# Squared-ReLU MLP's second half: quarter sums issued further ahead, left operands made in three steps, later weights' loads moved ahead and onto two queues

## The chip, the cores and the metric

The kernel runs on one core of one Trainium2 chip. A time is the device time of one execution in microseconds (us); the kernel before took 2211.32 us (median of 3 runs, 2208.41 to 2215.10). The core's engines are named as the profile names them: PE multiplies matrices (PEld loads its weights), DVE adds and subtracts, ACT copies, casts and applies functions, POOL here does little but issue DMAs, SP issues DMAs. Every engine has a queue of its own and works through it in order.

## The reference

One decoder layer on x of 512 rows by 2048 columns, all in float32:

```python
u = x * (1.0 + sc1) + sh1
y = _mixer(u, ...)                       # gated linear attention and mLSTM heads
x = _layer_norm(ALPHA * x + g1 * y, ln1_g, ln1_b)
u = x * (1.0 + sc2) + sh2
y = jnp.square(jax.nn.relu(u @ w_ff1)) @ w_ff2      # 2048 -> 8192 -> 2048
x = _layer_norm(ALPHA * x + g2 * y, ln2_g, ln2_b)
```

sh, sc and g come from the conditioning vector. The change is in the second product of the MLP, h² @ w_ff2, where h² is 512 by 8192 and w_ff2 is 8192 by 2048, and in the last steps of the first product, beside which the second one is begun.

## The kernel before

The layer is computed stage by stage: modulation, mixer, output projection and first norm; the MLP's first product, whose squared results go to DRAM (`hd`); the MLP's second product; the last norm. Float32 operands are split into two reduced-precision parts, hi and lo (lo is the operand less hi), and a product is three matmuls: hi by hi, hi by lo, lo by hi.

**The sevens.** The first twelve blocks of 512 hidden rows ("fours") are multiplied by a Strassen-Winograd scheme: a block of four quarter products is replaced by seven products of sums of quarters. The twelve fours are worked off in nine *runs* (runs 0 to 8), of 2, 3, 3, 3, 3, 3, 3, 3 and 1 fours and with the two halves of the output columns in turn. A run goes through seven *passes*, in the order of products 1, 2, 5, 7, 3, 6, 4 (`PASS`), and a pass takes each four of its run in turn. One four in one pass is a *unit*: 12 matmuls of 128x512 (`seven`, L1531 to L1538). There are NU = 168 units. A pass collects in two PSUM banks; after it ACT copies both to SBUF (`evac`, L1560, two copies) and a DMA adds them to `sums` in DRAM: the first time written by SP, then added by POOL (L1564).

**What a unit needs.** From the weights: the four quarters of a four come by SP (`quarter_load`, 512 KB each, L1315, into two rings of six). `right_operand` is called two units ahead of the matmuls (LOOK = 2). For products 5, 7, 6 and 4 it first has DVE make a sum of quarters in place (L1327), then ACT casts it to hi (L1330), then the pending subtractions are issued (`low_parts`), and the subtraction for this unit's lo (DVE, L1332) is put on the list `lows`, to be issued by the next call. hi and lo stand in rings of three. From the activations: `left_operand` makes two DVE sums for products 5 (L1292, L1293) and 3 (L1295, L1296), at once the ACT cast to hi (L1299), and puts the DVE subtraction for lo (L1300) on the same list. `WHEN` says in which pass each left operand is made, one step per unit.

**Order.** DVE and ACT run in the order in which the program calls them; PE, SP and POOL are ordered by a scheduler. At unit n the loop therefore puts on DVE, in this order: the sum of quarters for unit n + 2, if it wants one, the lo of unit n + 1, and what left operands are due; ACT gets the cast of unit n + 2, the left casts, and after a pass the two copies.

**The end of the first product.** After the last block of the first product, DVE and ACT combine seven PSUM banks (L1472 to L1488, seven DVE operations of 128x512), then apply relu and square (`waiting`, L1492) and store to `hd`. The quarters of run 0 are loaded there, and the first two fours' left operands are made beside it (`beside_last`).

**The plain part.** The other hidden rows: 24 *plain units* of 24 matmuls, in four column blocks C0 to C3 of six units (L1546 to L1548; weights loaded by `c_load`, L130, into a ring `raw` of three buffers that the activations `hr` also pass through, split by `split`, L125 on ACT and L126 on DVE). In C0 the sums of the sevens are read back from DRAM (`sums_load`, L1574, called q) and combined (`z_sums`). Then 192 matmuls of `last_sum`, the last norm, and the output.

Of the kernel before, what the change touches and what calls it, by code (L numbers as in the profile page):

```python
# [58 lines left out]
def trunk_layer_kernel(  # L59
# [1227 lines left out]

    def left_operand(f, k):
# [8 lines left out]
        src = q[{1: (1, 1), 2: (1, 2), 5: (2, 1), 7: (1, 1), 3: (1, 2), 6: (1, 1), 4: (2, 2)}[m]]
        h, l = (slot(HOME[kind_of(f)][1], f"a{f}_{m}{e}") for e in "hl")
        A.copy(halves(h), src)  # L1299
        lows.append(lambda: V.tensor_tensor(halves(l), src, halves(h), ALU.subtract))  # L1300
        left[f, m] = h, l
# [79 lines left out]
    WHEN = {"a": (1, 1, 4, 4, 7, 8, 8), "b": (4, 4, 7, 7, 8, 8, 8), "c": (4, 4, 4, 7, 7, 8, 8)}  # L1381

    def spread(r, k, fns):
        fs = len(runs[r])
        for i, fn in enumerate(fns):
            at(at_pass(r, k) + i * fs // len(fns), fn)
# [62 lines left out]
    for nb in range(2, DFF // CB):  # L1449
# [120 lines left out]
    def sums_load(h, j, q, k):  # L1570
# [185 lines left out]
```

## Time and profile before

| | us |
| --- | --- |
| median of 3 runs | 2211.32 (2208.41 to 2215.10) |
| the profiled execution, its own time | 2206.32 |
| its span in the trace | 2204.6 |
| PE busy in the span | 2111.1 (96%) |
| DVE busy in the span | 1718.5 (78%) |
| ACT busy in the span | 961.9 (44%) |
| sevens, runs 0 to 8 (1487.75 to 2006.88) | 519.13 |
| plain blocks C0 to C3 (2006.88 to 2147.86) | 140.98 |
| last sums and norm (from 2147.86) | 56.7 |

The span is what the trace covers; the execution's own time is 1.7 us longer, and the median of the three runs is 5.0 us above that execution. A row of a wait says which instruction stood idle, which instruction released it, the sum of these waits, their number and the longest. A row of a timeline says when an instruction began, how long it took from start to end (the next one can begin a little before that end, so the distance of two starts is what a queue pays), and in brackets how long its engine had been idle and what ended it.

### The profile page before, as it was taken

The page shows a single profiled execution, that of the slowest core. Times are in us where ns is not written, and L with a number is a line of the kernel's source. Part 1 is how long each engine was busy: PE and PEld are TensorE (multiplying, and loading weights), DVE is VectorE, ACT ScalarE, POOL GpSimd, SP SyncE. Part 2 cuts the span into 40 slices and gives each one's busy share as a digit, 9 for nine tenths or more (in the row PEclk, how much of TensorE's full clock was granted, in tenths as well). Part 3 has the DMA queues.
Part 4 walks back from the last instruction along what each step waited for, and adds up shares of the span by engine and source line. Part 5 has one row for each costly group of instructions (what it writes and reads, how often), then busy time and mean ns, then how long its engine had stood idle before and what let it go on. Part 6 is the DMA issues. An engine that isn't in the chain of part 4 may idle for free.

```text
span 2204.6 us, 30720 instructions
## 1 busy us (share of the span) xinstructions
PE 2111.1 (96%) x11857; PEld 1826.7 (83%) x11857; DVE 1718.5 (78%) x2550; ACT 961.9 (44%) x1328; POOL 166.1 (8%) x156
## 2 busy tenths in 40 slices
PE   6999999999999999999999999997999899998997
PEld 4777788888888879999999999995777687777786
DVE  7985777577777788987888878877777877775888
ACT  4223643343331145544544545445555555553233
POOL 3334101000000000000000000000001010001002
PEclk9999999999999999999999999999999999999999
DMA  8875444766678866444443444447467677769652
GB/s 312 285 266 172 137 144 147 245 201 228 223 256 290 287 204 201 131 139 123 143 128 113 154 125 129 140 155 273 171 175 185 175 196 176 192 169 262 220 179 79
DMA packets 187120, 415.04 MB, mean 188 GB/s; under 512 B 17105, under 2 KB 19373, under 8 KB 186973
## 3 DMA queue, kind: packets, MB, share of 16 engines
q1 hardware_dynamic: 179916, 387.38, 53.2%
q0 software_dynamic: 7056, 25.69, 7.0%
q8 instruction: 93, 1.52, 0.3%
q14 instruction: 55, 0.44, 0.1%
HBM read 354.74 MB, written 58.21 MB: 187 GB/s over the span
## 4 chain that ended last, share of the span: by engine, by line
PE 69%; DVE 14%; DMA 8%; ACT 5%; issue 3%; POOL 0%; SPq 0%; ACTq 0%; DVEq 0%; POOLq 0%
PE fp L1461 8%; PE fp L1460 8%; PE fp L1462 8%; PE gp L1537 4%; PE gp L1538 4%; PE gp L1536 4%; DMA wr<-in_w_ada_dram 3%; DVE wr L162 3%; DVE w L1327 2%; PE gp L1547 1%; PE gp L1548 1%; PE gp L1546 1%; PE wo_0b L228 1%; PE wo_0b L230 1%; PE wo_0b L229 1%
## 5 line engine op out<-in xcount | busy, mean ns | idle before, releaser
L162 DVE SCALAR_TENSOR_TENSOR wr<-wr,csb 128x1024 f32<-128x1024 f32 x192 | 257.7, 1362 | 24.2 <-DMA wr<-in_w_ada_dram 24.0
L1564 POOL DMA_DIRECT2D sums<-z x49 | 42.2, 861 | 1132.6 <-ACT z L1560 1120.1
L1327 DVE TENSOR_TENSOR w<-w,w 128x1024 f32<-128x1024 f32 x96 | 116.9, 1217 | 0.0
L1560 ACT COPY z<-gp 128x512 f32<-128x512 f32 x126 | 70.5, 587 | 26.5 <-PE gp L1538 14.5
L1169 DVE TENSOR_TENSOR z<-f 128x512 f32<-128x512 f32 x112 | 76.7, 685 | 3.1 <-DMA f<-in_w_ff_dram 3.1
L1332 DVE TENSOR_TENSOR w_3lo<-w,w_3hi 128x1024 fp32r<-128x1024 f32 x24 | 29.4, 1225 | 36.7 <-ACT w_3hi L1330 36.7
L1332 DVE TENSOR_TENSOR w_1lo<-w,w_1hi 128x1024 fp32r<-128x1024 f32 x24 | 29.4, 1225 | 29.4 <-ACT w_1hi L1330 27.9
L1492 ACT ACTIVATE z<-z 128x1024 f32<-128x1024 f32 x28 | 28.1, 1053 | 54.6 <-DVE z L1487 54.6
L1171 DVE TENSOR_TENSOR z<-f,z 128x256 f32<-128x256 f32 x112 | 47.6, 425 | 3.9
L1172 DVE TENSOR_TENSOR z<-f,z 128x256 f32<-128x256 f32 x112 | 47.6, 425 | 3.8
L1536 PE MATMUL gp<-w_5hi,a_5h 128*128 128x512 f32 x96 | 38.2, 424 | 8.7 <-ACT w_5hi L1330 8.7
L1537 PE MATMUL gp<-w_5lo,a_5h 128*128 128x512 f32 x96 | 39.8, 415 | 6.6 <-DVE w_5lo L1332 6.6
L1537 PE MATMUL gp<-w_6lo,a_6h 128*128 128x512 f32 x96 | 38.4, 400 | 5.3 <-DVE w_6lo L1332 5.3
L1536 PE MATMUL gp<-w_3hi,a_3h 128*128 128x512 f32 x96 | 37.8, 398 | 5.4 <-ACT w_3hi L1330 5.4
L1536 PE MATMUL gp<-w_4hi,a_4h 128*128 128x512 f32 x96 | 37.8, 397 | 5.1 <-ACT w_4hi L1330 5.1
L1330 ACT CAST w_5hi<-w 128x1024 fp32r<-128x1024 f32 x24 | 25.2, 1051 | 37.2 <-DVE w L1327 37.2
L1537 PE MATMUL gp<-w_2lo,a_2h 128*128 128x512 f32 x96 | 38.5, 402 | 2.8 <-DVE w_2lo L1332 2.8
L1330 ACT CAST w_6hi<-w 128x1024 fp32r<-128x1024 f32 x24 | 25.3, 1052 | 34.7 <-DVE w L1327 34.7
L1536 PE MATMUL gp<-w_7hi,a_7h 128*128 128x512 f32 x96 | 37.7, 394 | 2.5 <-ACT w_7hi L1330 2.5
L1538 PE MATMUL gp<-w_5hi,a_5l 128*128 128x512 f32 x96 | 39.2, 409 | 0.0
L1537 PE MATMUL gp<-w_4lo,a_4h 128*128 128x512 f32 x96 | 37.6, 391 | 1.1 <-DVE w_4lo L1332 1.1
L1537 PE MATMUL gp<-w_7lo,a_7h 128*128 128x512 f32 x96 | 37.6, 391 | 1.1 <-DVE w_7lo L1332 1.0
(1849 smaller groups left out, 8024.2 us busy)
## 6 DMA issues: line engine op xcount, KB each, us to landing
wr<-in_w_ada_dram SPq DMA_DIRECT2D x192, 512.0 KB, 4.7
f<-in_w_ff_dram SPq DMA_DIRECT2D x136, 512.0 KB, 3.7
w<-in_w_ff_dram SPq DMA_DIRECT2D x96, 512.0 KB, 6.5
sums<-z POOLq DMA_DIRECT2D x49, 512.0 KB, 6.5
hd<-z SPq DMA_DIRECT2D x32, 512.0 KB, 4.1
z<-hd SPq DMA_DIRECT2D x12, 1024.0 KB, 7.4
sums<-z SPq DMA_DIRECT2D x14, 512.0 KB, 2.9
q<-sums SPq DMA_DIRECT2D x12, 512.0 KB
```

Of the source, the lines that this page charges most:

```text
L162: V.scalar_tensor_tensor(raw, raw, 1.0, csb[:, h * DH:(h + 1) * DH], ALU.mult, ALU.mult, accum_out=msum[:, h, v * KT + k:v * KT + k + 1])
L1169: V.tensor_tensor(halves(f[:, :S]), halves(raw[:, HB:3 * HB]), b12.unsqueeze(1).to_broadcast([P, 2, HB]), ALU.add)
L1327: V.tensor_tensor(q[o], q[x], q[o], ALU.add)
L1330: A.copy(h, src)
L1332: lows.append(lambda: V.tensor_tensor(l, src, h, ALU.subtract))
L1460: T.matmul(o, lhsT=wh[:, sl], rhs=q[:, 0], start=i == 0 and j == 0, stop=False)
L1461: T.matmul(o, lhsT=wh[:, sl], rhs=q[:, 1], start=False, stop=False)
L1462: T.matmul(o, lhsT=wl[:, sl], rhs=q[:, 0], start=False, stop=i == KP - 1 and j == 1)
L1536: T.matmul(pb[j], lhsT=qh[:, sl], rhs=wh[:, e], start=first and e == 0, stop=False)
L1537: T.matmul(pb[j], lhsT=qh[:, sl], rhs=wl[:, e], start=False, stop=False)
L1538: T.matmul(pb[j], lhsT=ql[:, sl], rhs=wh[:, e], start=False, stop=last and e == 1)
L1560: A.copy(st_[:, j * CB:(j + 1) * CB], pb[j])
```

## The change

Six things move. None adds or removes a matmul, a sum or a DMA's bytes.

1. **Sums of quarters** leave `right_operand`. `sums_at` lists for each unit n the sums that are issued there: those of unit n + 4 in runs of three fours (n + 3 in run 0, n + 2 in run 8). `right_sums(n)` stands behind `prepare2`, so a sum follows the lo of the unit n + 1.
2. **Left operands** go through `left_step`, once a unit: the lows of the step before, then the casts staged by the step before, then the new sums or casts. Sums and casts of products 5 and 3 so lie one step apart, and the lo another.
3. **Start.** Behind the last block of the first product, p1's copy is followed by the loads of the quarters and the first cast of the sevens; h2's copy and the combination come behind, the lo and the sums of run 0 are woven into them, and relu and square are taken at units 1 and 2 in place of 2 and 4.
4. **Loads of quarters** (1,2) and (2,2) are called 3 and 1 units ahead of a run of three fours (before 1 ahead, 2 behind).
5. **Plain loads** are called three ahead in place of two, the first three at run 8's units 0, 1, 2; the activations `hr` of the last part and its weights `wl` are loaded ahead into the rings of the quarters.
6. **The loads of q** are issued by POOL in place of SP; those of the first quarter two units later.

The core of the diff:

```diff
     def left_operand(f, k):
         q, m = fours[f], PASS[k]
-        low_parts()
+        src = q[{1: (1, 1), 2: (1, 2), 5: (2, 1), ...}[m]]
+        def high():
+            h, l = (slot(HOME[kind_of(f)][1], f"a{f}_{m}{e}") for e in "hl")
+            A.copy(halves(h), src)
+            left[f, m] = h, l
+            stage["low"].append(lambda: V.tensor_tensor(halves(l), src, halves(h), ALU.subtract))
+        if m not in (5, 3):
+            return high()
...
+        stage["high"].append(high)
+
+    def left_step(*new):
+        lo, hi = stage["low"], stage["high"]
+        stage.update(low=[], high=[])
+        for fn in lo + hi + list(new):
+            fn()
...
     def right_operand(r, k, e):
         m = PASS[k]
-        if len(runs[r]) == 1:
-            low_parts()
-        for m_, o, x in ((5, (1, 1), (1, 2)), (7, (1, 2), (2, 2)), (6, (1, 1), (2, 2)),
-                         (4, (1, 1), (2, 1))):
-            if m == m_:
-                V.tensor_tensor(q[o], q[x], q[o], ALU.add)
...
+    for n, (_, r, k, e) in enumerate(units[:NU]):
+        sums_at.setdefault(max(0, n - min(4, len(runs[r]) + 1)), []).append((r, k, e))
...
-        c_load(c + 2)
+        c_load(c + 3)
...
-    WHEN = {..., "c": (4, 4, 4, 7, 7, 8, 8)}
+    WHEN = {..., "c": (4, 4, 4, 7, 8, 8, 8)}
...
-        lead = (8, 5, 1, -2) if len(fs) > 1 else (8, 5, 3, 2)
+        lead = (8, 5, 3, 1) if len(fs) > 1 else (8, 5, 3, 2)
...
         A.copy(p1, pb[1])
-        A.copy(h2[:, :, lo_], pb[3])
-        V.tensor_tensor(h1[:, :, lo_], p1, pb[2], ALU.add)
...
             prepare2(LOOK)
+        A.copy(h2[:, :, lo_], pb[3])
+        V.tensor_tensor(h1[:, :, lo_], p1, pb[2], ALU.add)
+        if nb == DFF // CB - 1:
+            low_parts()
...
+        if nb == DFF // CB - 1:
+            right_sums(0)
...
-        nc.sync.dma_start(t[:, :n], src[:, k:k + n, j])
+        G.dma_start(t[:, :n], src[:, k:k + n, j])
...
+        if n >= NU - 7 - LOOK:
+            low_parts()
+            right_sums(n)
         if n:
             prepare2(n + LOOK)
-        if n in (2, 4):
+            right_sums(n)
+        if n in (1, 2):
             waiting.pop(0)()
+        left_step(*lefts.pop(n, ()))
```

How DVE's queue stands at the begin of run 2, the first even run of three fours. `w_e_Mlo` is the lo of four e of the run in product M, `w_e_ij` a quarter (the row with two quarters on the right is the sum), `a_Ml` a left lo, `z<-z` a left sum. Before:

```order
1751 L1327 TENSOR_TENSOR w_2_11_15022<-w_2_12_15165,w_2_11_15022 128x1024
1752 L1300 TENSOR_TENSOR a_4l<-z,a_4h 128x512
1753 L1332 TENSOR_TENSOR w_0_5lo<-w_2_11_15022,w_0_5hi 128x1024
1754 L1295 TENSOR_TENSOR z<-z 128x2x256
1755 L1296 TENSOR_TENSOR z<-z 128x2x256
1756 L1300 TENSOR_TENSOR a_3l<-z,a_3h 128x512
1757 L1327 TENSOR_TENSOR w_3_11_15045<-w_3_12_15194,w_3_11_15045 128x1024
1758 L1300 TENSOR_TENSOR a_6l<-z,a_6h 128x512
1759 L1332 TENSOR_TENSOR w_1_5lo<-w_3_11_15045,w_1_5hi 128x1024
```

And after:

```order
1746 L1346 TENSOR_TENSOR w_1_2lo<-w_3_21_15108,w_1_2hi 128x1024
1747 L1337 TENSOR_TENSOR w_3_11_15046<-w_3_12_15151,w_3_11_15046 128x1024
1748 L1299 TENSOR_TENSOR a_5l<-z,a_5h 128x512
1749 L1299 TENSOR_TENSOR a_7l<-z,a_7h 128x512
1750 L1346 TENSOR_TENSOR w_2_2lo<-w_4_21_15131,w_2_2hi 128x1024
1751 L1337 TENSOR_TENSOR w_4_11_15071<-w_4_12_15169,w_4_11_15071 128x1024
1752 L1299 TENSOR_TENSOR a_6l<-z,a_6h 128x512
1753 L1299 TENSOR_TENSOR a_4l<-z,a_4h 128x512
1754 L1307 TENSOR_TENSOR z<-z 128x2x256
1755 L1308 TENSOR_TENSOR z<-z 128x2x256
1756 L1346 TENSOR_TENSOR w_0_5lo<-w_2_11_15022,w_0_5hi 128x1024
```

The sum for four 1 of product 5 stood two rows ahead of its lo and now stands a whole pass ahead of it; the two left sums stand behind the lows that were staged.

DVE's queue at the begin of run 0 (L1474 to L1488 before and L1505 to L1515 after are the combination of the first product's banks). Before:

```order
1650 L1474 TENSOR_TENSOR z<-z,fp_2_13896 128x2x256
1651 L1475 TENSOR_TENSOR z<-z,fp_6_13900 128x512
1652 L1476 TENSOR_TENSOR z<-z,fp_7_13898 128x512
1653 L1477 TENSOR_TENSOR z<-z,fp_5_13899 128x512
1654 L1486 TENSOR_TENSOR z<-fp_5_13899,z 128x2x256
1655 L1487 TENSOR_TENSOR z<-z 128x2x256
1656 L1488 TENSOR_TENSOR z<-z,fp_4_13901 128x2x256
1657 L1332 TENSOR_TENSOR w_0_2lo<-w_0_21_14385,w_0_2hi 128x1024
1658 L1300 TENSOR_TENSOR a_7l<-z,a_7h 128x512
1659 L1332 TENSOR_TENSOR w_1_2lo<-w_1_21_14387,w_1_2hi 128x1024
```

And after:

```order
1647 L1505 TENSOR_TENSOR z<-z,fp_2_13896 128x2x256
1648 L1346 TENSOR_TENSOR w_0_2lo<-w_0_21_14375,w_0_2hi 128x1024
1649 L1508 TENSOR_TENSOR z<-z,fp_6_13900 128x512
...
1654 L1515 TENSOR_TENSOR z<-z,fp_4_13901 128x2x256
1655 L1299 TENSOR_TENSOR a_5l<-z,a_5h 128x512
1656 L1337 TENSOR_TENSOR w_0_11_14246<-w_0_12_14379,w_0_11_14246 128x1024
1657 L1299 TENSOR_TENSOR a_3l<-z,a_3h 128x512
1658 L1299 TENSOR_TENSOR a_7l<-z,a_7h 128x512
1659 L1307 TENSOR_TENSOR z<-z 128x2x256
1660 L1308 TENSOR_TENSOR z<-z 128x2x256
1661 L1346 TENSOR_TENSOR w_1_2lo<-w_1_21_14377,w_1_2hi 128x1024
```

The first lo of product 2 has moved ahead of six combinations; the second one has moved from two rows behind the first to twelve rows behind.

POOL's queue from run 7 on after the change (sums_14399 and sums_14400 are the two column halves); before, it held the accumulations alone:

```order
86 L1598 DMA sums_14399<-z 128x1024 x3
87 L1608 DMA q_0_0_18071<-sums_14399 128x2x512
88 L1598 DMA sums_14399<-z 128x1024 x3
89 L1608 DMA q_0_4_18096<-sums_14399 128x2x512
90 L1608 DMA q_0_2_18131<-sums_14399 128x2x512
91 L1608 DMA q_1_0_18133<-sums_14399 128x2x512
92 L1598 DMA sums_14399<-z 128x1024
93 L1598 DMA sums_14400<-z 128x1024 x4
94 L1608 DMA q_0_6_18168<-sums_14399 128x512
95 L1598 DMA sums_14400<-z 128x1024
96 L1608 DMA q_1_4_18172<-sums_14399 128x2x512
```

Four reads of the sums now stand ahead of run 7's last accumulation, and two more between those of run 8.

## Rows read from the trace of the kernel before

**Rows 1.** Page, part 1: busy time, share of the span, instructions.
```profile
PE 2111.1 (96%) x11857; PEld 1826.7 (83%) x11857; DVE 1718.5 (78%) x2550; ACT 961.9 (44%) x1328; POOL 166.1 (8%) x156
```

**Rows 2.** Windows: us; busy (instructions) PE, PEld, DVE, ACT, POOL; PEclk, DMA share, GB/s.
```profile
1487.75:1544.21 56.46, 43.94 (x170) 32.92 (x169) 41.37 (x47) 30.81 (x44) 0.00 (x0) 0.91 0.78 275
1544.21:1605.39 61.18, 58.41 (x253) 46.79 (x252) 47.60 (x47) 34.53 (x46) 0.00 (x0) 1.00 0.54 186
1605.39:1670.62 65.23, 60.57 (x253) 47.88 (x252) 50.87 (x52) 35.03 (x47) 5.34 (x6) 0.97 0.66 173
...
1923.42:1986.74 63.32, 58.22 (x253) 46.99 (x252) 48.31 (x50) 37.44 (x52) 6.00 (x7) 1.00 0.74 185
1986.74:2006.88 20.14, 19.63 (x85) 15.55 (x84) 13.50 (x12) 13.02 (x21) 5.15 (x6) 1.00 1.02 244
2006.88:2047.73 40.85, 35.20 (x145) 28.30 (x144) 16.94 (x22) 8.87 (x11) 1.71 (x2) 0.92 0.84 259
2047.73:2082.58 34.85, 32.94 (x146) 26.95 (x144) 32.67 (x47) 7.28 (x8) 0.00 (x0) 1.00 0.75 246
2082.58:2115.22 32.64, 32.64 (x146) 27.03 (x144) 28.60 (x41) 8.58 (x10) 0.00 (x0) 1.00 0.53 171
```

**Rows 3.** Windows, PE alone: a pass of run 2 without a wait.
```profile
1644.56:1652.72 8.16, 8.16 (x38) 1.00 0.74 186
```

**Rows 4.** Waits of PE in runs 2 and 3, 1605.39 to 1731.76.
```profile
PE gp L1536 <- ACT w_5hi L1330: 2.4, 1, 2.4
```

**Rows 5.** Waits of ACT in the same stretch.
```profile
ACT w_5hi L1330 <- DVE w L1327: 9.6, 6, 2.1
```

**Rows 6.** Timeline of DVE in run 2: start, duration, instruction.
```profile
1615.53 1.23 DVE L1332 TENSOR_TENSOR w_2lo<-w,w_2hi 128x1024 fp32r<-128x1024 f32 x1 [0.26 <-ACT w_2hi L1330]
...
1623.27 0.69 DVE L1295 TENSOR_TENSOR z<-z 128x512 f32<-128x512 f32 x1
1623.99 0.69 DVE L1296 TENSOR_TENSOR z<-z 128x512 f32<-128x512 f32 x1
...
1630.66 0.68 DVE L1300 TENSOR_TENSOR a_4l<-z,a_4h 128x512 fp32r<-128x512 f32 x1
1631.26 1.22 DVE L1327 TENSOR_TENSOR w<-w,w 128x1024 f32<-128x1024 f32 x1
1632.40 1.22 DVE L1332 TENSOR_TENSOR w_5lo<-w,w_5hi 128x1024 fp32r<-128x1024 f32 x1
...
1643.12 1.23 DVE L1332 TENSOR_TENSOR w_3lo<-w,w_3hi 128x1024 fp32r<-128x1024 f32 x1 [1.45 <-ACT w_3hi L1330]
1646.32 1.23 DVE L1332 TENSOR_TENSOR w_3lo<-w,w_3hi 128x1024 fp32r<-128x1024 f32 x1 [1.97 <-ACT w_3hi L1330]
```

**Rows 7.** Timeline of ACT in run 2, at the end of a unit.
```profile
1642.04 1.05 ACT L1330 CAST w_3hi<-w 128x1024 fp32r<-128x1024 f32 x1 [1.62 <-PE gp L1538]
```

**Rows 8.** Timeline of PE in run 2, a unit's second matmul.
```profile
1616.82 0.50 PE L1537 MATMUL gp<-w_2lo,a_2h 128*128 128x512 f32 x1 [0.16 <-DVE w_2lo L1332]
```

**Rows 9.** Timeline of DVE at run 0's begin.
```profile
1491.55 0.68 DVE L1474 TENSOR_TENSOR z<-z,fp 128x512 f32<-128x512 f32 x1
```

**Rows 10.** Timeline of PE in run 0: the two long waits.
```profile
1497.25 0.54 PE L1537 MATMUL gp<-w_2lo,a_2h 128*128 128x512 f32 x1 [2.34 <-DVE w_2lo L1332]
...
1524.82 1.22 PE L1536 MATMUL gp<-w_3hi,a_3h 128*128 128x512 f32 x2 [5.35 <-ACT w_3hi L1330]
```

**Rows 11.** Waits of ACT in run 0, 1487 to 1545.
```profile
ACT z L1560 <- DMA hd<-z: 7.5, 1, 7.5
```

**Rows 12.** Waits of PE in run 8 and C0, 1985 to 2062.
```profile
PE gp L1546 <- ACT f_3hi L125: 5.2, 1, 5.2
```

**Rows 13.** Waits of SP's queue in the same stretch.
```profile
SPq L1574 <- DMA sums<-z: 7.3, 1, 7.3
```

**Rows 14.** DMA issues, 1985 to 2035: transfer, KB, us to landing.
```profile
q<-sums SPq DMA_DIRECT2D x2, 256.0 KB, 24.1
```

**Rows 15.** Page, part 6: the quarters' loads.
```profile
w<-in_w_ff_dram SPq DMA_DIRECT2D x96, 512.0 KB, 6.5
```

More of the change, by code (lines that the diff above doesn't have):

```diff
@@ L1286, in fetch_four @@
         fours[f] = {(1 + o, 1 + t): v[:, :, t, o] for t in range(2) for o in range(2)}
+    stage = {"high": [], "low": []}
     def left_operand(f, k):
         q, m = fours[f], PASS[k]
-        low_parts()
+        src = q[{1: (1, 1), 2: (1, 2), 5: (2, 1), 7: (1, 1), 3: (1, 2), 6: (1, 1), 4: (2, 2)}[m]]
+        def high():
[5 more added lines that the diff above has]
+            return high()
         if m == 5:
@@ L1293, in left_operand @@
             V.tensor_tensor(q[2, 1], q[2, 1], q[2, 2], ALU.subtract)
-        if m == 3:
+        else:
             V.tensor_tensor(q[1, 1], q[1, 1], q[2, 2], ALU.subtract)
             V.tensor_tensor(q[1, 2], q[1, 2], q[1, 1], ALU.add)
[L1297 to L1301, printed above, removed]
+        stage["high"].append(high)
[4 more added lines that the diff above has]
+            fn()
     quarters = {}
@@ L1316, in quarter_load, with right_sum @@
         quarters[r, e, i, j] = t
+    SUM = {5: ((1, 1), (1, 2)), 7: ((1, 2), (2, 2)), 6: ((1, 1), (2, 2)), 4: ((1, 1), (2, 1))}
+    def right_sum(r, k, e):
+        if PASS[k] in SUM:
+            o, x = (quarters[r, e, *q] for q in SUM[PASS[k]])
+            V.tensor_tensor(o, x, o, ALU.add)
     def right_operand(r, k, e):
         m = PASS[k]
-        q = {(i, j): quarters[r, e, i, j] for i in (1, 2) for j in (1, 2)
-             if (r, e, i, j) in quarters}
-        if len(runs[r]) == 1:
-            low_parts()
-        for m_, o, x in ((5, (1, 1), (1, 2)), (7, (1, 2), (2, 2)), (6, (1, 1), (2, 2)),
-                         (4, (1, 1), (2, 1))):
-            if m == m_:
-                V.tensor_tensor(q[o], q[x], q[o], ALU.add)
-        src = q[{1: (1, 1), 2: (2, 1), 5: (1, 1), 7: (1, 2), 3: (2, 2), 6: (1, 1), 4: (1, 1)}[m]]
+        src = quarters[r, e, *{1: (1, 1), 2: (2, 1), 5: (1, 1), 7: (1, 2), 3: (2, 2), 6: (1, 1),
+                               4: (1, 1)}[m]]
         h, l = (strm.tile([P, 2, CB], F32R, tag=g, name=f"w{r}_{e}_{m}{g}") for g in ("hi", "lo"))
@@ L1333, in right_operand, with right_sums, h_fetch @@
         ahead.append((h, l))
-    hraws, craws, hops = {}, {}, {}
-    def h_fetch(ft):
-        hraws[ft] = strm.tile([P, 2, S], F32, tag="raw", bufs=3, name=f"hr{ft}")
+    sums_at = {}
+    for n, (_, r, k, e) in enumerate(units[:NU]):
+        sums_at.setdefault(max(0, n - min(4, len(runs[r]) + 1)), []).append((r, k, e))
+    def right_sums(n):
+        for u in sums_at.pop(n, ()):
+            right_sum(*u)
+    hraws, craws, hops = {}, {}, {}
+    def h_fetch(ft, pool=None):
+        if pool:
+            hraws[ft] = pool.tile([P, 2, S], F32, tag="b1", bufs=6, name=f"hr{ft}")
+        else:
+            hraws[ft] = strm.tile([P, 2, S], F32, tag="raw", bufs=3, name=f"hr{ft}")
         r0 = ft % 4 * P
@@ L1377, in prepare2 @@
             w_plain(n - NU)
[L1381 to L1386, printed above, removed]
+    WHEN = {"a": (1, 1, 4, 4, 7, 8, 8), "b": (4, 4, 7, 7, 8, 8, 8), "c": (4, 4, 4, 7, 8, 8, 8)}
     todo = {}
@@ L1400, in trunk_layer_kernel @@
                            3 if kind_of(f) == "a" else 2), lambda f=f: fetch_four(f))
+    lefts = {}
     for (r, k), fns in todo.items():
-        spread(r, k, fns)
+        fs = len(runs[r])
+        for i, fn in enumerate(fns):
+            lefts.setdefault(at_pass(r, k) + i * fs // len(fns), []).append(fn)
     for r, fs in enumerate(runs):
-        lead = (8, 5, 1, -2) if len(fs) > 1 else (8, 5, 3, 2)
+        lead = (8, 5, 3, 1) if len(fs) > 1 else (8, 5, 3, 2)
         for (i, j), d in zip(((1, 1), (2, 1), (1, 2), (2, 2)), lead):
@@ L1413, in trunk_layer_kernel @@
         at(R7 + n, lambda i=i: c_pair(i))
-    for c in range(2):
-        at(R8 + 1 + 2 * c, lambda c=c: c_load(c))
+    for c in range(3):
+        at(R8 + c, lambda c=c: c_load(c))
     ahead, waiting = [], []
@@ L1433, in beside_last @@
             quarter_load(0, i - 5, 1, 1)
-        for f, ks in ((a, {4: 0, 5: 1, 7: 2}), (b, {4: 0, 5: 1, 6: 2, 7: 3})):
-            if i in ks:
-                left_operand(f, ks[i])
+        new = {4: ((a, 0), (b, 0)), 5: ((a, 1), (b, 1)), 6: ((b, 2),), 7: ((a, 2), (b, 3))}
+        if i in new:
+            left_step(*(lambda u=u: left_operand(*u) for u in new[i]))
         if i == KP - 1:
-            left_operand(b, 4)
             low_parts()
+            left_step(lambda: left_operand(b, 4))
     LOOK = 2
@@ L1588, in z_sums @@
         yield
-    for h, j, n0, n1 in ((0, 0, -4, 0), (0, 1, 0, 3), (1, 0, 5, 7), (1, 1, 10, 12)):
+    for h, j, n0, n1 in ((0, 0, -2, 1), (0, 1, 0, 3), (1, 0, 5, 7), (1, 1, 10, 12)):
         q = {}
@@ L1620, in trunk_layer_kernel @@
                 for i_ in range(2):
+                    at(n + 1 + i_, lambda i=i_: h_fetch(tail + 2 * i, ff3))
                     at(n + 3 + 2 * i_, lambda i=i_: tail_h(i))
             if b == 2:
+                for i_ in range(2, 8):
+                    at(n + 2 + i_, lambda i=i_: tail_fetch(i // 2, i % 2))
                 for i_ in range(2):
+                    at(n + i_, lambda i=i_: tail_fetch(0, i))
                     at(n + 1 + 2 * i_, lambda i=i_: tail_w(0, i))
```

15 lines of the change are left out of this document (9 added, 6 removed).

## The prediction

> **What bounds the kernel now.** The page's busy times come first: PE is busy 2111.1 of 2204.6 us [rows 1], so only idle or slow PE can be won back, and the windows by run say where [rows 2]. A wait-free pass gives the measure: 8.16 us for three units [rows 3], 2.72 a unit, 0.227 a matmul; a plain block without waits takes 32.64 [rows 2]. So a run of three fours could last 21 x 2.72 = 57.12, run 0 with 14 units 38.08, run 8 with 7 units 19.04. Against that the windows [rows 2] hold: run 0 56.46, excess 18.4; run 1 61.18, excess 4.1, and runs 3 and 5 like it; run 2 65.23, excess 8.1, and runs 4 and 6 like it; run 7 63.32, excess 6.2; run 8 20.14, excess 1.1; C0 40.85, excess 8.2; C1 34.85, excess 2.2; C2 none. Together 18.4 + 3 x 4.05 + 3 x 8.1 + 6.2 + 1.1 + 8.2 + 2.2 = 72.6 us: all that the change can reach.
>
> The waits say why. In runs 2 and 3 PE's largest wait is for the cast of a product-5 hi [rows 4], and ACT in turn waited 9.6 us in six waits for DVE's sum of quarters [rows 5]: the sum stands right ahead of the cast that needs it, behind whatever DVE has queued. DVE is busy 50.87 of 65.23 us there [rows 2]; it is not short of time over a run, but of time at one place. The odd runs' clock stays at 1.00, the even ones show 0.97, run 0 0.91 [rows 2]: after a long wait matmuls run at half clock, which makes run 0's PE busy 43.94 instead of 38.08, 5.9 us more.
>
> **Prices on DVE's queue.** What a queue pays is the distance between starts [rows 6]: a sum or a lo 1.14 (1631.26 to 1632.40), a left lo 0.60 (I use 0.61), the first left sum 0.72 and, by the same form, 0.61 for the second, together 1.33. Over two runs DVE needs 24 + 42 sums and lows at 1.14, 21 left lows and 6 pairs of left sums: 75.2 + 12.8 + 8.0 = 96 of 114.2 us, 84%. It fits on the mean; the question is the bursts.
>
> **When a lo must start.** hi and lo rings have three buffers, so the cast for unit u starts when unit u - 3 ends: 1642.04 against 1641.84, one unit before the pass boundary at 1644.56 [rows 3, 7]. The lo follows 1.08 later, at 1643.12 [rows 6], 1.28 behind the unit's end; with the evacuation's copies in between, at 1646.32, 1.76 behind the boundary. From the lo's start to the unit's second matmul, which uses it, pass 1.29 us (1615.53 to 1616.82) [rows 6, 8]. With time counted from a run's start, the lo of unit u may start no earlier than 2.72(u - 2) + 1.28 (1.76 after a pass), and must start by 2.72u + 0.23 - 1.29 = 2.72u - 1.06.
>
> **Parts 1 and 2, sums and left operands.** With the sum a pass ahead, ACT's wait for it goes; what is late next is the lo, behind sums and left work in the new order.
> - Odd runs: from unit 3 on (start 4.00) rows cost 2.28, 3.61, 2.89 by units 3, 4, 5; unit 4 starts at its earliest, 6.72, unit 5 at 10.33, unit 6 at 13.22 against 15.26 allowed. Unit 7: 17.33 against 17.98, unit 8: 20.22 against 20.70. No wait: excess 0 (0 to 0.2 with full durations, 1.22 and 0.68, in place of distances).
> - Even runs: unit 2 starts at 1.76; the queue then holds 2.47 (a lo, two left sums), 2.89, 3.50 and 4.83 (a lo, a sum, two left lows, two left sums), and DVE is never idle: unit 6 at 15.45 against 15.26, unit 7 at 18.34 against 18.17 with the 0.19 already lost, unit 8 at 21.84 against 21.06. Lost 1.1, with the restarts 1.3 a run; 0 at best, 3 with full durations. Waits this short cost no clock in the odd runs of before.
> - Run 7 has the splits of the plain part's activations besides, whose subtraction waits for ACT: by the same walk 2.0 in product 5 and 0.8 in product 6, 2.8 (0 to 4.5).
>
> **Part 3, run 0.** The lo of its first product-2 unit no longer stands behind six combinations, so the 2.34 us wait [rows 10] goes; and relu and square come earlier, so `hd` is stored earlier, ACT's 7.5 us wait for that store [rows 11] goes, and with it PE's 5.35 [rows 10]. But the second lo of product 2 now stands behind it by six combinations, a sum, three left lows and two left sums. The first combination starts at 1491.55 [rows 9]; the first lo then at 1492.2, its successors at 1493.3, and 11 operations at about 0.62 and one of 1.14, 8.0 us, put the second lo at 1501.3, its matmul at 1502.6. Without the wait PE is done with the unit before at about 1494.9 + 2.5 = 1497.4 and has three matmuls that need no lo, to 1498.1. PE stands 4.5 to 5.2 us; I take 5.0 (4 to 6.4). Half clock behind it: 5.9 us went with before's two long waits and some small ones, so 1.9 for one; small waits 0.5. Run 0: 5.0 + 1.9 + 0.5 = 7.4 (4 to 9).
>
> **Part 4, quarters' loads.** They land 6.5 us after issue [rows 15] and go out earlier than before; they cost nothing while they arrive before their sum, which is itself earlier now (last rival).
>
> **Parts 5 and 6, run 8 and C0.** Before, PE waits 5.2 us in C0 for the cast of the fourth plain weight [rows 12], whose load was issued by SP late: SP stood 7.3 us at a load of q that waited for an accumulation [rows 13]. On POOL's queue that load holds up nobody's weights. It holds up accumulations instead: four reads stand ahead of run 7's last one, so a staging buffer comes free later and ACT's copy waits; with four buffers and passes of 2.72 us I put this at 1.1 us on top: run 8 2.2 (1 to 4). In C0 the DMA engines remain: run 8 and C0 hold 20.14 x 1.02 + 40.85 x 0.84 = 54.9 us of full DMA time [rows 2], while without PE's waits they last 19.04 + 32.64 = 51.7. 3.2 do not fit; a part can go to C1, so C0 keeps 2.0 (0 to 8.2), C1 0 (0 to 2.2).
>
> The Trainium skill, "Trainium Kernel Development and Optimization", section Key Constraints, says that DMAs issued from SP's, ACT's and POOL's queues run on the same 16 DMA engines and interleave, so that several issuers save only issue time. By that rule two queues bring nothing where the DMA engines are full, as the share of 1.02 in run 8 suggests; the 7.3 us that SP stood speak for a queue held up at its head, which the rule leaves out. By the rule the sum would be the third rival's.
>
> **Sum.** Left over: 7.4 + 0 + 3 x 1.3 + 2.8 + 2.2 + 2.0 = 18.3 of 72.6, a gain of 54.3. The profiled execution took 2206.3, so 2152.0; it lies 5.0 below the median of the runs, which I add: 2157.0.
>
> **Rivals.**
> - *No new wait* (0.13): DVE's queue runs as its mean of 84% allows, run 0 keeps 4, nothing else remains: gain 68.6, 2143. For it: odd runs keep 0.5 to 2 us of margin. Against: the second lo in run 0 stands twelve rows back.
> - *The DMA engines, not the queue, bound C0* (0.14): the 8.2 + 2.2 stay, in place of 2.0: 8.4 more, 2165. For it: DMA shares 1.02 and 0.84 [rows 2]. Against: SP's 7.3 us of standing [rows 13].
> - *DVE's bursts cost their full durations* (0.10): even runs 3, odd 0.2, run 7 4.5: 1.7 x 3 + 0.6 + 1.7 = 7.4 more, 2164; with a half clock behind each, up to 2175.
> - *Quarters late at the new sum* (0.05, the other side): product 5's first sum is now issued at 5.4 into a run (lo of unit 3 at 4.2 plus 1.14). It adds quarter (1,2), whose buffer comes free with the run before's product-4 cast and lo, at the earliest 11.1 us ahead of the run's start: 16.5 us for a load. The median is 6.5, but loads took 24.1 where accumulations and loads meet [rows 14]. DVE would then stand with every lo behind that sum. A landing of 24.1 costs 7.6 in each of eight runs, 61 us: 2152 + 61 + 5 = 2218. It eats the gain from landings of about 23 us on. Against: runs 1 to 7 show DMA shares of 0.54 to 0.74, not 1.02.
> - *The waits only change their names* (0.03): each sum taken off ACT's wait is found again in the lo's wait, 2205 to 2215.
>
> **How the numbers follow.** The forecast, 2157, has 0.55. The range 2141 to 2179 takes in the first three rivals, the low ends together (4 + 0 + 0 + 0 + 1 + 0 leaves 5: 2144) and the high ends (9 + 0.6 + 9 + 4.5 + 4 + 8.2 + 2.2 = 37.5: 2176), and leaves out the last two. 0.3% of 2211 is 6.6 us, about what a measurement of this kernel can tell from no change. Faster by more: 0.55 + 0.13 + 0.14 + 0.10 = 0.92; within: 0.03; slower: 0.05.
>
> **What would show it.** Right: odd runs of about 57.2 us and even ones of 58.4 at a granted clock of 1.00; no wait of a cast for a sum of quarters in them; in the even runs short waits of PE for the lows of product 5; run 0 of about 45.5 with one wait of some 5 us at the second unit of product 2; C0 of about 34.6 without the wait for the fourth plain cast. Wrong: even runs over 60 (DVE's bursts are dearer); a wait of DVE's sums for loads in every run (the quarters are late); PE's wait for the fourth plain weight still there, now for its load (the DMA engines bound it); run 8 over 24 us (POOL's queue costs more than a buffer's turn); run 0 over 50.

## The result and the profile after

The changed kernel takes 2151.16 us (median of 4 runs, 2149.66 to 2158.69) against 2210.38 of the kernel before (4 runs, 2208.41 to 2215.10): ratio 0.9736, 95% interval 0.9708 to 0.9764. The forecast was 2157.0, the range 2141 to 2179. The profiled execution took 2152.55 us, its span is 2150.8, 53.8 shorter than before's.

Windows of the changed kernel by run, as in [rows 2]: runs 0, 1, 2, 7, 8, then C0 and C1 (runs 3 and 5 repeat run 1, runs 4 and 6 repeat run 2).

```profile
1489.84:1533.84 44.00, 40.53 (x171) 32.51 (x169) 39.44 (x45) 30.73 (x42) 0.00 (x0) 0.96 0.95 335
1533.84:1590.96 57.12, 57.12 (x254) 47.30 (x252) 47.38 (x48) 34.84 (x46) 0.00 (x0) 1.00 0.65 222
1590.96:1648.60 57.64, 57.64 (x254) 47.09 (x252) 50.06 (x52) 35.04 (x47) 5.38 (x6) 1.00 0.78 201
...
1878.04:1937.42 59.38, 57.77 (x254) 47.11 (x252) 48.16 (x50) 37.47 (x52) 6.79 (x8) 1.00 0.78 192
1937.42:1959.79 22.37, 19.83 (x86) 15.40 (x84) 12.30 (x12) 11.74 (x18) 7.77 (x10) 1.00 0.99 271
1959.79:1996.20 36.41, 35.93 (x145) 29.14 (x145) 24.63 (x33) 11.37 (x15) 7.92 (x12) 0.91 0.92 279
1996.20:2028.84 32.64, 32.64 (x146) 27.03 (x144) 26.91 (x38) 6.33 (x6) 1.64 (x3) 1.00 0.78 264
```

Run 1 lasts 57.12 us, the wait-free 21 x 2.72 to the hundredth, and run 2 57.64 where it took 65.23. In runs 2 and 3 no wait of PE is listed any more, and the largest wait of ACT, 9.6 us for sums of quarters before [rows 5], is now one for PE itself, which is a reserve (waits of ACT):

```profile
ACT z L1594 <- PE gp L1572: 12.1, 13, 1.6
```

The half us that an even run keeps lies at the lows of product 5, in delays of about 0.1 us that are too short for that list: the second matmul below begins 0.35 us behind the first, in place of 0.23 (timeline of PE in run 2).

```profile
1607.28 0.39 PE L1570 MATMUL gp<-w_5hi,a_5h 128*128 128x512 f32 x1
1607.63 0.50 PE L1571 MATMUL gp<-w_5lo,a_5h 128*128 128x512 f32 x1
```

Most of what is left lies at three places. In run 0 PE's two waits, and DVE's lo that ends the second (timeline of PE, then of DVE):

```profile
1500.38 0.50 PE L1570 MATMUL gp<-w_5hi,a_5h 128*128 128x512 f32 x1 [1.74 <-ACT w_5hi L1344]
1502.57 0.80 PE L1571 MATMUL gp<-w_2lo,a_2h 128*128 128x512 f32 x1 [1.69 <-DVE w_2lo L1346]
```
```profile
1501.30 1.22 DVE L1346 TENSOR_TENSOR w_2lo<-w,w_2hi 128x1024 fp32r<-128x1024 f32 x1
```

In run 7 the lo of product 5 (waits of PE in that run), and between run 8 and C0 the first plain cast (timeline of PE; the wait stands ahead of C0's first matmul, so it counts in run 8):

```profile
PE gp L1571 <- DVE w_5lo L1346: 1.3, 1, 1.3
```
```profile
1959.79 0.78 PE L1580 MATMUL gp<-f_0hi,hb 128*128 128x512 f32 x1 [2.07 <-ACT f_0hi L125]
```

The last one has to do with POOL's queue. In its timeline three reads of q stood 8.85 us (the row names a load of x as what they waited for), and behind them run 7's last accumulation, whose copy ACT had begun at 1936.94, goes out at 1942.42 together with run 8's first:

```profile
1930.53 0.84 POOL L1598 DMA_DIRECT2D sums<-z  x1 [8.09 <-ACT z L1594]
1940.21 2.21 POOL L1608 DMA_DIRECT2D q<-sums  x3 [8.85 <-DMA x<-xd]
1942.42 1.91 POOL L1598 DMA_DIRECT2D sums<-z  x2
```

It reaches ACT as a wait of the copy for its staging buffer, behind which f_0's cast is queued (waits of ACT, 1937 to 2000; PE, which the row names, had long ended that pass):

```profile
ACT z L1594 <- PE gp L1572: 3.9, 1, 3.9
```

In the trace that copy begins at 1957.71, just behind the landing of run 8's first accumulation at 1957.64. This one went out within 1 us of its own copy's end, but took 14.6 us to land; with q on ACT (below) the same one took 7.4 (DMA issues, here and in that run):

```profile
sums<-z POOLq DMA_DIRECT2D x1, 512.0 KB, 14.6
```
```profile
sums<-z POOLq DMA_DIRECT2D x1, 512.0 KB, 7.4
```

### The profile page after: what moved, and what is told of

The parts are those of the page before. It is cut to its first block, busy times and chain, and to the rows that moved or that the text cites. A ratio compares the mean times of both kernels' runs of the same rounds, so it can differ in the third digit from the quotient of the medians.

```text
span 2150.8 us, 30715 instructions
## 1 busy us (share of the span) xinstructions
PE 2096.5 (97%) x11857; PEld 1826.9 (85%) x11857; DVE 1714.2 (80%) x2550; ACT 964.0 (45%) x1328; POOL 178.8 (8%) x172
## 4 chain that ended last, share of the span: by engine, by line
PE 82%; DVE 9%; DMA 5%; ACT 2%; issue 2%; POOL 0%; SPq 0%; DVEq 0%; ACTq 0%; POOLq 0%
PE fp L1484 9%; PE fp L1483 9%; PE fp L1485 9%; PE gp L1571 7%; PE gp L1572 6%; PE gp L1570 6%; DVE wr L162 3%; DMA wr<-in_w_ada_dram 3%; PE gp L1581 2%; PE gp L1582 2%; PE gp L1580 2%; PE wo_0b L228 1%; PE wo_0b L230 1%; PE wo_0b L229 1%; PE mv0b L228 1%
## 5 line engine op out<-in xcount | busy, mean ns | idle before, releaser
L1572 PE MATMUL gp<-w_2hi,a_2l 128*128 128x512 f32 x96 | 38.1, 397 | 0.0
L1346 DVE TENSOR_TENSOR w_4lo<-w,w_4hi 128x1024 fp32r<-128x1024 f32 x24 | 28.7, 1221 | 11.4 <-ACT w_4hi L1344 11.4
L1570 PE MATMUL gp<-w_2hi,a_2h 128*128 128x512 f32 x96 | 37.5, 392 | 0.0
L1572 PE MATMUL gp<-w_6hi,a_6l 128*128 128x512 f32 x96 | 37.4, 389 | 0.0
L1570 PE MATMUL gp<-w_1hi,a_1h 128*128 128x512 f32 x96 | 37.4, 389 | 0.0
```

The lines of the kernel that those rows point to most:

```text
L1570: T.matmul(pb[j], lhsT=qh[:, sl], rhs=wh[:, e], start=first and e == 0, stop=False)
L1572: T.matmul(pb[j], lhsT=ql[:, sl], rhs=wh[:, e], start=False, stop=last and e == 1)
```

## The experiments

Times of whole executions of one kernel often spread by 5 us and more. Part of that lies ahead of everything changed: in the profiled executions the sevens began between 1487.8 and 1499.2 us, while the first product ahead of them lasted 563.16 us in each. Below, each kernel's profile is therefore read by its excess: the length of a stage less 2.72 us a unit (5.44 a plain unit). It repeats to 0.1 us in runs 1 to 7. The intervals of all the kernels between 2147 and 2157 overlap; what is said of these kernels rests on the stages.

| kernel | median us | ratio to before (95%) | run 0 | runs 1 to 7 | run 8 | C0, C1 |
| --- | --- | --- | --- | --- | --- | --- |
| before | 2210.4 | | 18.4 | 42.7 | 1.1 | 10.4 |
| changed | 2151.2 | 0.9736 (0.9708 to 0.9764) | 5.9 | 3.7 | 3.3 | 3.8 |
| changed, again | 2152.7 | 0.9729 (0.9707 to 0.9751) | 6.5 | 3.7 | 2.5 | 2.8 |
| sums late | 2154.4 | 0.9735 (0.9709 to 0.9760) | 7.4 | 7.8 | 2.3 | 2.8 |
| left at once | 2181.6 | 0.9858 (0.9832 to 0.9884) | 10.0 | 23.1 | 2.5 | 2.8 |
| before + sums ahead | 2182.1 | 0.9864 (0.9840 to 0.9888) | 17.2 | 19.6 | 1.1 | 9.7 |
| before + three steps | 2171.8 | 0.9810 (0.9779 to 0.9840) | 8.1 | 8.1 | 1.1 | 10.7 |
| before + cast later | 2166.2 | 0.9796 (0.9760 to 0.9833) | 11.9 | 8.0 | 1.1 | 9.6 |
| q on SP | 2157.3 | 0.9748 (0.9725 to 0.9770) | 6.7 | 3.7 | 1.1 | 8.8 |
| q on ACT | 2152.0 | 0.9728 (0.9693 to 0.9762) | 5.9 | 3.7 | 1.1 | 0.0 |
| plain loads back | 2153.9 | 0.9734 (0.9705 to 0.9763) | 6.7 | 3.8 | 1.5 | 1.2 |
| begin, first try | 2149.5 | 0.9715 (0.9685 to 0.9744) | 6.5 | 3.7 | 1.4 | 1.2 |
| begin, second try | 2150.1 | 0.9715 (0.9688 to 0.9742) | 4.4 | 3.7 | 5.1 | 0.0 |
| second try, q on ACT | 2147.4 | 0.9706 (0.9682 to 0.9730) | 4.4 | 3.7 | 1.1 | 0.0 |

**Sums late.** From the changed kernel:
```diff
-        sums_at.setdefault(max(0, n - min(4, len(runs[r]) + 1)), [])...
+        sums_at.setdefault(max(0, n - 2), [])...
...
+        right_sums(n)
         if n:
             prepare2(n + LOOK)
-            right_sums(n)
```


> The changed kernel with one part undone: each sum of quarters is issued right before the cast that needs it, two units ahead, as before; the left operands keep their three steps. Theory A (the place of the sum decides): ACT's casts wait for sums again, the odd runs of three fours show an excess of 3 to 4 us over 57.12, the even ones 3 to 8, run 7 4 to 6; in all 25 to 35 us, about 2180. Theory B (the three steps of the left operands took the waits away, the sums' place is secondary): the runs keep their length, under 5 us in all, about 2155.

Theory A fell and theory B came out. With the sums back at their old place the odd runs stay at 57.12, the even ones at 57.7 to 57.8; only run 7's excess goes from 2.26 to 5.9. 4.1 us in runs 1 to 7 is all that the sums' place is worth once the rest of the change is there.

**Left at once.** From the changed kernel, `stage["high"].append(high)` becomes `high()`, the lo goes on the list `lows`, and `low_parts()` stands ahead of the left sums. `WHEN` stays as changed.

> The changed kernel with one part undone: the left operands' sums are followed at once by their cast and, at the next unit, by their lo; the sums of quarters stay ahead. Theory A (the sums' place decides; the three steps only smooth): the odd runs stay at 57.1 to 58, the even ones rise from 57.6 to 58.5 to 60, 4 to 9 us in all, about 2157. Theory B (three steps are half of the gain): even runs of 62 and more, over 15 us in all, 2167 and more.

Theory A fell here too, and theory B came out: even runs of 62.2 to 63.8, odd ones of 58.4, 19.4 us in runs 1 to 7 and 4 in run 0; the medians are some 30 us apart, the rest lies ahead of the sevens (they begin 3 us later) and in the spread of the executions. That `WHEN` has product 3's operand made a pass later for the fours of kind c is thus not what helps.

**Before with the sums ahead, and before with the three steps.** Each half of the pair alone:

> The kernel before with one part alone: the sums of quarters issued up to four units ahead; left operands, run 0's begin, the plain part's loads and q stay as before. Theory A: runs 1 to 7, which had 42.6 us of excess, keep 5 to 12; run 0 (18.4), run 8, C0 and C1 (11.5) stay: about 2178. Theory B (the parts work only together): runs 1 to 7 keep over 25 us, 2195 and more.

> The kernel before with the three-step left operands alone; sums of quarters right before their cast, run 0's begin, the plain part's loads and q as before. Theory C (the waits were a ping-pong of two queues: ACT stood at a left cast for a DVE sum, DVE at a lo for ACT's next cast; either part breaks it): runs 1 to 7, 42.6 us of excess before and 19.6 with the sums alone, keep 5 to 10; odd runs 0 to 0.5, even ones 0.5 to 1.5, run 7 5 to 6; run 0, run 8, C0, C1 keep about 30; about 2176. Theory D (the new begin or the loads helped the runs too): over 15 in runs 1 to 7, 2185 and more.

The first gave 23.1 of the 42.7 us, the second 34.6, and in the changed kernel 39.0 are gone: the two cures overlap. The sums alone keep 19.6 us, which is between the two theories, so neither of them came out. In runs 1 to 7 the three steps came out as theory C said: odd runs 57.12, even ones 57.7 to 58.0, run 7 63.0. Now the rows. In the kernel before, ACT waited in runs 2 and 3 not only for sums of quarters [rows 5] but also, 7.9 us each, for the left sums of products 3 and 5 (waits of ACT, before):

```profile
ACT a_3h L1299 <- DVE z L1296: 7.9, 3, 2.6
ACT a_5h L1299 <- DVE z L1293: 7.9, 3, 2.6
```

With the three steps alone these two waits are gone. ACT still waits for sums of quarters, 6.6, 4.2 and 1.7 us in runs 2 and 3 (waits of ACT), and PE hardly stands (waits of PE, windows of runs 1 and 2). The 1.7 are what is left of the 9.6 of [rows 5], with the sums at their old place:

```profile
ACT w_7hi L1343 <- DVE w L1340: 6.6, 4, 2.3
ACT w_4hi L1343 <- DVE w L1340: 4.2, 3, 1.8
...
ACT w_5hi L1343 <- DVE w L1340: 1.7, 2, 1.3
```
```profile
PE gp L1547 <- ACT w_7hi L1343: 0.2, 1, 0.2
```
```profile
1543.00:1600.12 57.12, 57.12 (x253) 47.31 (x252) 47.10 (x48) 34.92 (x46) 0.00 (x0) 1.00 0.57 198
1600.12:1657.91 57.79, 57.55 (x254) 47.16 (x252) 49.87 (x52) 35.26 (x47) 5.32 (x6) 1.00 0.76 200
```

With the sums ahead alone it is the reverse: ACT waits for no sum of quarters, but 10.6 and 8.6 us for left sums (waits of ACT, runs 2 and 3), the lo behind it comes late, and PE waits (waits of PE; window of run 2):

```profile
ACT a_3h L1299 <- DVE z L1296: 10.6, 3, 5.3
...
ACT a_5h L1299 <- DVE z L1293: 8.6, 3, 3.4
```
```profile
PE gp L1545 <- DVE w_5lo L1332: 1.8, 2, 1.4
PE gp L1544 <- ACT w_5hi L1330: 0.9, 1, 0.9
```
```profile
1600.58:1662.78 62.20, 58.78 (x254) 46.86 (x252) 50.61 (x52) 34.49 (x47) 5.33 (x6) 1.00 0.71 186
```

The expectation was wrong for run 0: it let run 0, run 8, C0 and C1 keep about 30 us with the three steps alone, and they keep 19.9, since run 0 falls from 18.4 to 8.1. There the combination, relu and square stand in their old places, but the left operands made beside the last block go in three steps too. The first combination starts at 1496.77, with the sevens' first matmul at 1496.79 (before it stood 3.8 us behind it), and the lo of product 2 costs PE 0.2 us (timeline of DVE; waits of PE and of ACT in run 0):

```profile
1496.77 0.68 DVE L1485 TENSOR_TENSOR z<-z,fp 128x512 f32<-128x512 f32 x1
```
```profile
PE gp L1548 <- DVE w_2lo L1345: 0.2, 1, 0.2
```
```profile
ACT z L1571 <- DMA hd<-z: 4.3, 1, 4.3
```

**Cast later.** The same as the three steps, but the lo goes the old way (`lows.append`), so that of the left operands only the cast is moved a step. As in the three steps, `left_operand` no longer calls `low_parts` ahead of its sums:

> As the run with the left operands alone, but only their cast is put one step behind their sums; the lo goes out with the next unit's lows, as before. Theory C (what hurt was ACT standing at the left cast while the next weights' cast waited behind it): within 4 us of the run with all three steps. Theory E (what hurt was the left lo standing in DVE's queue ahead of a sum or a weights' lo): runs 1 to 7 keep 20 us and more, 12 us slower than the three steps.

Runs 1 to 7 keep 8.0 us as with all three steps (window of run 2 below), so the lo's own step is not needed there. What counts is that ACT does not stand at a left cast for DVE while the next weights' cast waits behind it. Two things in this edit can do that, the cast's later place and the weights' lo that no longer stands ahead of the left sums; they were not run apart. In run 0 the lo's step does count: 11.9 us here, 8.1 with it. The medians lie 5.6 us apart, the other way and more than the expected 4, with overlapping intervals; from the sevens' first matmul on this run takes 2.7 us longer, so that difference lies ahead of them and in the spread.

```profile
1597.66:1655.41 57.75, 57.50 (x253) 47.16 (x252) 49.88 (x52) 35.26 (x47) 5.33 (x6) 1.00 0.76 205
```

**q on SP.** `G.dma_start` is `nc.sync.dma_start` again:

> The changed kernel with the loads of q back on SP's queue and everything else kept. Theory A (a queue held up at its head): without the reads of q among them the accumulations go out as they come, run 8 falls from 22.4 to about 20.2, but SP stands at a read of q ahead of plain loads and C0 rises from 36.4 to 38 to 41; net 0 to 3 us slower, about 2153. Theory B (the DMA engines bound this stretch, whoever issues): run 8 and C0 together stay within 1 us of 58.8, 2151. Theory C (POOL's queue is a loss altogether): run 8 20.2 and C0 34 to 35, 4 us faster, 2147.

Theory A by its mechanism, and a little over its numbers: run 8 20.14, C0 41.44, the median 2157.3. SP stands 6.8 us at a read of q, and PE's wait for the fourth plain cast is back with the 5.2 us of [rows 12] (waits of SP, of PE):

```profile
SPq L1608 <- DMA sums<-z: 6.8, 1, 6.8
```
```profile
PE gp L1580 <- ACT f_3hi L125: 5.2, 1, 5.2
```

**q on ACT.**
```diff
-        G.dma_start(t[:, :n], src[:, k:k + n, j])
+        nc.scalar.dma_start(t[:, :n], src[:, k:k + n, j])
...
-    for h, j, n0, n1 in ((0, 0, -2, 1), (0, 1, 0, 3), (1, 0, 5, 7), (1, 1, 10, 12)):
+    for h, j, n0, n1 in ((0, 0, 0, 2), (0, 1, 1, 3), (1, 0, 5, 7), (1, 1, 10, 12)):
```


> The changed kernel with the reads of q issued by ACT at their place in the program, all of the first ones behind run 8's last accumulation, and the sums made from the first quarter one unit later. Theory A (queues held up at their head): POOL's accumulations go out as they come, run 8 falls from 22.4 to 20.2; SP has no q, C0 falls from 36.4 to 33 to 35; 4 us faster, 2147. Theory B (the DMA engines are full there, whoever issues): run 8 and C0 together stay within 1.5 us of 58.8.

The profile gives theory A more than it asked for: run 8 20.15, C0 32.64 without any wait (windows below), 52.8 us for the two against 58.8. The edit does two things: the reads change queue, and they go out later. None of them lies in run 8 here (4 in the changed kernel), 9 lie in C0 as there, and the DMA engines moved 14.3 MB in the 52.8 us where they had moved 16.2 in 58.8, at nearly the same rate. So shares of 1.02 and 0.94 do not by themselves make PE wait; whether the queue or the later place did it is open, since POOL with the reads at the later place was not run. In the whole time the gain does not show: 2152.0, intervals overlapping; from the sevens' first matmul to the end of the span it is 655.1 against 661.0.

```profile
1936.52:1956.67 20.15, 19.66 (x86) 15.56 (x84) 13.50 (x12) 13.45 (x21) 5.61 (x7) 1.00 1.02 240
1956.67:1989.31 32.64, 32.64 (x146) 27.04 (x144) 17.78 (x23) 9.69 (x13) 1.23 (x2) 1.00 0.94 290
```

**Plain loads back.** `c_load(c + 2)`, and the first two at run 8's units 1 and 3:

> The changed kernel with the plain loads called two ahead again, two first ones at run 8's units 1 and 3; q stays on POOL, the tail's loads stay ahead. Theory A (SP's queue was held by q, not by the loads' distance): C0 within 2 us of the changed kernel's 36.4, run 8 within 1 of 22.4, the total within 3 us, 2149 to 2154. Theory F (the loads' distance is the gain): PE waits again for the fourth plain weight, C0 39 to 42, 2155 to 2158.

Theory A, and beyond its bounds on the short side: run 8 20.58, C0 33.80. That they are shorter than the changed kernel's cannot be told from the spread: with q on POOL the excess of the two was 7.1 and 5.3 in the changed kernel's two profiles, 5.1, 5.3, 2.6 and 5.1 in four kernels with the same loads, and 2.7 here. No gain of the loads' distance shows. The loads of quarters called earlier were not run alone, but the runs with the three steps alone (without them) and with the sums late (with them) differ by only 0.3 us in runs 1 to 7.

**Begin, first try.** Four of the six combinations are moved behind the second lo of product 2 and the first sum, relu and square one unit later:

> The changed kernel with run 0's second product-2 lo and the first sum put ahead of four of the six combinations, relu and square one unit later. Theory A (that lo's place sets run 0's wait): run 0's excess falls from 5.9 to 1 to 2.5 and the half clock behind it goes, 3.5 to 5 us faster, 2147. Theory B (what comes later then hurts: relu, square and the store to DRAM, for which the copies of the passes wait): run 0's excess stays at 5 and more, only at later passes.

That lo's wait went and another came, as theory B has it, and run 0 keeps 6.5, though not for relu: the first pass's copy waits 5.46 us for the last combination, since its staging buffer holds p1 and u2, and product 5's cast is queued behind it (timeline of ACT):

```profile
1499.70 1.07 ACT L1599 COPY z<-gp 128x512 f32<-128x512 f32 x2 [5.46 <-DVE z L1515]
```

**Begin, second try, alone and with q on ACT.** Beside the order told in the expectation, run 0's left operands of products 3, 6 and 4 are made three units later here. Those of its second four for products 6 and 4 then read a buffer that holds the next four already: these two kernels compute other values there, with as many instructions, and their times stand for the order alone. A kernel that keeps the values in this order was not run.

> The changed kernel with run 0's begin in a new order: two combinations, then the lows and sums of products 2 and 5 each as early as their cast allows, the other four combinations between them, the new left operands three units later, relu and square at units 3 and 4, and the first four passes' copies in the two staging buffers that the combinations and relu do not hold. Theory A (each wait of run 0 is one instruction standing too far back in a queue): run 0's excess 5.9 falls to 0.5 to 2.5, 3.5 to 5 us faster than the changed kernel. Theory B (DVE has too much to do there, whatever the order): excess 4 and more, the wait only moves to a later pass.

> The same new begin together with the reads of q on ACT. Theory A: run 0 0.5 to 2.5, runs 1 to 7 3.7 as in the changed kernel, run 8 1.1, C0 0 to 0.5: from the sevens' first matmul to the end about 651 us against 661 of the changed kernel, the median about 2142. Theory B: one of the two gives its gain back, 655 and more.

Run 0 keeps 4.4, in waits of 1 us and less at four places (waits of PE in the first of the two, window of run 0 in the second):

```profile
PE gp L1581 <- ACT w_6hi L1344: 1.0, 1, 1.0
PE gp L1582 <- DVE w_7lo L1346: 0.6, 1, 0.6
```
```profile
1490.92:1533.38 42.46, 39.83 (x170) 30.85 (x169) 39.50 (x45) 30.40 (x42) 0.00 (x0) 1.00 0.96 334
```

Theory B by its number: no longer one wait, but 1.5 to 2 us is all that the order gave back. The granted clock of run 0 is 1.00, and DVE is busy 39.5 of the 42.5 us. With q on ACT the sum of excesses is 9.2, and the span from the sevens on 653.5, between the 651 of theory A and the 655 of theory B; the median is 2147.4 where 2142 was expected.

**The changed kernel again.**

> The changed kernel itself once more, on the same chip as the run with both. Its time should lie within 4 us of 2151. What varies from execution to execution lies ahead of the sevens (their first matmul came between 1488 and 1497 us so far) and in run 8 with C0 (5.1 to 7.1 us of excess where q is on POOL); runs 1 to 7 should repeat to 0.1 us.

2152.69, as expected; runs 1 to 7 repeat, run 8 and C0 do not (2.5 and 2.8 for 3.3 and 3.8). On this chip the run with both was 5.3 us faster, 2147.41, with intervals of the ratio that overlap (0.9682 to 0.9730 and 0.9707 to 0.9751).

## Why the prediction came out, step by step

- **The sum.** Left over were 18.3 us by the forecast; the profile shows 5.9 + 1.5 (three even runs) + 2.26 + 3.3 + 3.8 = 16.8. From the sevens' first matmul to the end the changed kernel is 55.9 shorter, its whole span only 53.8, because the sevens begin 2.1 later; the first product's first matmul is late by the same 2.09, so that came from ahead of anything changed. The forecast for the profiled execution was 2152.0, it took 2152.55.
- **The 5.0 us from the profiled execution to the median** did not repeat: the changed kernel's median lies 1.4 below its profiled execution. This is the term behind nearly all of the 5.8 us between forecast and result.
- **DVE's queue.** Odd runs 0, measured 0; even 1.3, measured 0.5; run 7 2.8, measured 2.26. The walk with start distances came within 0.8 us a run, and product 5 was the right place.
- **The cause of the waits was read wrongly.** The step "the waits say why" took ACT's wait for a sum of quarters [rows 5] for the reason why PE waits. With the three steps alone that wait falls from 9.6 to 1.7 us though the sums stand where they stood, and 10.8 us of such waits for products 7 and 4 remain with PE nearly unharmed. What the runs show is two queues that stop each other: ACT stands at a left cast until DVE comes to the left sums, DVE has weights' work ahead of them, and the cast that the next lo needs is queued behind on ACT. The weights' work is more than the section on the kernel before says: `left_operand` begins with `low_parts`, so the lo of the very unit whose cast ACT has just been given (`w_0_5lo` in the order before) stands ahead of the left sums. Moving the sums of quarters takes 23.1 of 42.7 us away, the three steps 34.6. The forecast was saved by pricing parts 1 and 2 together, as one walk through the new order; theory A, which is this reading, failed in each of the three runs that split them (sums late, left at once, sums ahead alone).
- **Run 0.** 7.4, measured 5.9. The two waits of [rows 10] went, but not by part 3 alone, as the prediction had it: the three steps with the old combination take run 0 from 18.4 to 8.1, and about 2 us are left for the new begin. The wait for `hd` falls there from 7.5 to 4.3 without relu and square being earlier. With the new begin the lo of the second product-2 unit is the one that is late, at 1501.30 and its matmul at 1502.57, forecast 1501.3 and 1502.6. That the hour is met is chance: the stage began 2.1 later, the first combination started with it and not 3.8 us behind, and the first lo then waited for its quarter's load (ACT's cast stood 2.81 us for it). PE's stall, 3.4 in two waits, was shorter than 5.0; the half clock behind it was as priced.
- **Run 8 and C0.** 2.2 + 2.0, measured 3.3 + 3.8. The mechanism was seen (reads ahead of run 7's last accumulation, a staging buffer late), but its price was put in run 8 alone; the copy that waits holds the first plain cast, so C0 pays too, with a half clock (0.91). The buffer came late because an accumulation took 14.6 us to land, not because POOL issued it late. How much of that is the order in POOL's queue and how much the load of the DMA engines, the runs do not separate. The second rival (the paragraph on the rule calls it the third) had the waits of C0 and C1 stay; there the measurement decides: 10.4 us of excess before, 8.8 with q back on SP, 0.0 with q on ACT and later, at shares of 1.02 and 0.94 in run 8 and C0.
- The Trainium skill, "Trainium Kernel Development and Optimization", section Key Constraints, says that DMAs issued from several engines' queues run on the same 16 DMA engines and interleave. The shares of 1.02 and 0.94 in run 8 and C0 with q on ACT do not contradict that.
- **Part 5** was credited together with part 6. With part 5 kept and q back on SP 8.8 of the 10.4 us are there again, so most of it goes with q; the other 1.6 (C1's 2.2 are gone, C0 has 0.6 more) are not explained. **Part 4** was costed at nothing, and no gain of it shows.
- **Late quarters.** No sum waits for a load in runs 1 to 7. The 24.1 us that this rival feared are a read of q [rows 14]; plain weights landed in 7.5 in the same view.

## What to carry to other kernels

When two engines work through their queues in order and hand work to each other, look for the instruction that stands at the head of one queue while what the other needs is behind it; the largest wait in the list may be harmless. Put a cast one step behind the sum it reads, and price a new order by walking the queue with start-to-start distances. A read that waits for a write belongs on a queue, and at a place in it, where nothing urgent stands behind it.

## What the runs showed of the hardware

- With the same order on POOL's queue run 8 and C0 took 7.1 and 5.3 us of excess in two profiled executions of the changed kernel, and 2.6 in the first try of the begin. What differed is how long run 8's first accumulation took to land: 14.6, 13.6 and 12.3 us.
- A wait of 2.07 us ahead of C0's first matmul was followed by a dozen matmuls 0.43 us apart in place of 0.23, so it cost about 3 us more than itself. The granted clock was 0.50 there, the lower of its two levels (1.2 GHz), and 1.00 behind (timeline of PE; windows):

```profile
1962.07 0.63 PE L1580 MATMUL gp<-f_0hi,ha 128*128 128x512 f32 x1
1962.49 0.63 PE L1581 MATMUL gp<-f_0lo,ha 128*128 128x512 f32 x1
```
```profile
1959.79:1966.33 6.54, 6.06 (x13) 4.41 (x14) 2.54 (x3) 4.04 (x6) 2.67 (x4) 0.50 1.06 253
1966.72:1996.20 29.48, 29.48 (x132) 24.40 (x130) 21.71 (x31) 7.33 (x9) 5.14 (x8) 1.00 0.89 286
```
- A row of waits that names an engine long done (PE, for the copy that stood 3.9 us) stood for a buffer whose DMA had not landed: the copy began 0.07 us behind that landing.
